# Hybrid S5/MoBA decoder trunk on one core: the 12 table loads of the front in another order and at other steps

## The chip, the core and the metric

One core of a Trainium2 chip runs the whole trunk in one launch. The metric is the device time of the launch in microseconds; lower is better. The engines are named as in the profile: PE is TensorE (PEld its weight loads), DVE is VectorE, ACT is ScalarE, POOL is GpSimd, SP is SyncE, which issues most of the DMAs.

## The reference

Two layers work on x of 256 tokens by 1024 channels in float32. Each layer adds half a SwiGLU feed-forward, then a token mixer, then half a second feed-forward. Layer 0 mixes with a diagonal state-space layer (S5), layer 1 with block-sparse attention.

```python
def swiglu(h, w_gate, w_up, w_down):
    return (jax.nn.silu(h @ w_gate) * (h @ w_up)) @ w_down

for layer in range(DEPTH):
    h = h + 0.5 * swiglu(rms_norm(h, ffn_norm[layer, 0]), ...)
    h = h + mixer(rms_norm(h, mix_norm[layer]))
    h = h + 0.5 * swiglu(rms_norm(h, ffn_norm[layer, 1]), ...)
```

The part of the S5 mixer that matters here doesn't depend on x. Its state matrix, its B (64 groups x 64 states x 16 inputs, real and imaginary) and its C (64 x 16 x 64, real and imaginary) are turned into tables:

```python
    lam_re = mag * jnp.cos(a_im * dt)
    lam_im = mag * jnp.sin(a_im * dt)
    ...
    bb_re, bb_im = cmul(coef_re[..., None], coef_im[..., None], b_re.astype(f32), b_im.astype(f32))
```

## The kernel before

Every product is made of three fp32r matmuls: the activations and the weights are each split into a high part and the remainder, and high x high, high x low and low x high are added up (`mm3`). So each weight is read from DRAM once, as a "raw" tile of 128 x 2048 floats (1 MB), and split by two instructions for each half of it: ACT writes the high part (`whi`, L86) and DVE the rest (`wlo`, L87).

**The stream of weights.** `Stream` holds three raw buffers. The load of a raw is issued on SP's queue as soon as, in program order, the second half of the raw three places before it has been split (`free_raw`, called at the end of `split`); on the chip SP waits there for DVE's `wlo` of that half. Eight, later nine, pairs of split halves may be waiting for TensorE. `pump` splits the next half if a pair of buffers is free and if the raw was issued at least 8 steps ago.

**The first feed-forward.** `ffn` walks over 11 groups of 256 hidden columns. For group j the raws are (j,0) and (j,1), with the gate columns and the up columns of the upper and lower 512 input rows (two DMAs each, L176), and dj, the 256 rows of the down weights (one DMA, L182). For each group there are two products `gu(j, t)` for the two halves t of the tokens, eight steps of three matmuls (L399 to L401) each; behind each of them come ACT's `sg` (L480) and DVE's `act` (L484); `tr(j, t)` transposes the activations on TensorE (L497) in the middle of the next product, and ACT and DVE split them (L499, L500). `dn(j, f)` multiplies by half f of dj's rows into four banks. The order on TensorE is gu(1,0), gu(1,1), dn(0,0), gu(2,0), dn(0,1), gu(2,1), dn(1,0), gu(3,0), dn(1,1), gu(3,1), dn(2,0), and so on.

**The tables, woven in.** `tables` is a generator that builds the S5 tables during the first feed-forward. A clock counts steps: `fill(0.7)` is called before each of the eight steps of a `gu` and after each of the four banks of a `dn`, so a `gu` is 5.6 steps of the clock, a `dn` 2.8 and a whole group 16.8. Each call runs one turn of the loop at the end of `tables`. In a turn, all loads whose entry in `LOADS` is due are issued on SP; one transpose on TensorE is emitted if due (list `later`, from step 44); and the vector work in `work` is emitted if it is due and if the credit of DVE time allows it. All engines run their instructions in program order, so a load is issued behind every load that stands before it in the program.

The 12 loads are: `ld_b4(i, c)`, a quarter c of B, real (i = 0) or imaginary (i = 1), 64 KB in runs of 16 floats, into `bn` (L649); `ld_c2(i, a)`, half of C, 128 KB in runs of 64 floats, into `cn` (L654). Who reads them: `c_tr` transposes C on TensorE (L826), four times, at steps 44.1 to 48.3, and ACT copies the result (`cb`, L829). `b_all` multiplies `bn` by the coefficients on DVE (L628, z<-bn), first at step 49.0 in dn(1,1): one product that reads the real half and one that reads the imaginary half.

Counted out by the clock, the loads stand here before the change (B0r is the first quarter of B, real; C0r the first half of C, real):

| step | place on TensorE | loads |
|---|---|---|
| 16.1, 16.8 | end of gu(1,0) | B0r, B0i; raw d1 is issued after these |
| 17.5 to 19.6 | first four steps of gu(1,1) | B1r, B1i, B2r, B2i, B3r, B3i; raw (3,0) after these |
| 22.4 | end of gu(1,1) | C0r; raw (3,1) after it |
| 24.5, 26.6 | dn(0,0), gu(2,0) | C0i, C1r; raw d2 after them |
| 28.7 | gu(2,0) | C1i; raw (4,0) after it |

After raw (4,0) the kernel issues the second layer norm's gains and the rest of the constants (L290, L291), at step 30.1; then follow raws (4,1), d3, (5,0) at steps 36.4, 39.2 and 42.0.

Of the kernel before, what the change touches and what calls it, by code (L numbers as in the profile page):

```python
# [29 lines left out]
AO = (68, 68, 68, 68)  # L30
OO = 68

LOADS = (16, 16.5, 17, 17.5, 18, 18.5, 19, 19.5, 22, 24, 26, 28)
C_AT, E_AT, B_AT, DENSE, LAG, PACE, AGE = 44, 26, 36, 0.46, 12, 4.0, 8.0


# [84 lines left out]
def trunk_kernel(ctx: ExitStack, tc, x, ffn_norm, ffn_w_gate, ffn_w_up, ffn_w_down, mix_norm,  # L121
# [498 lines left out]
    def tables(tp):  # L620
# [26 lines left out]
        def ld_b4(i, c):  # L647
            b = (s5_b_re, s5_b_im)[i]
            nc.sync.dma_start(bn[i][:, 8 * c:8 * c + 8], bass.AP(tensor=b.tensor, offset=b.offset + 16384 * c,  # L649
                                                                 ap=[[16, 128], [2048, 8], [1, 16]]))  # L650

        def ld_c2(i, a):
            c = (s5_c_re, s5_c_im)[i]
            nc.sync.dma_start(cn[:, i, 4 * a:4 * a + 4], bass.AP(tensor=c.tensor, offset=c.offset + 32768 * a,  # L654
                                                                 ap=[[64, 128], [8192, 4], [1, 64]]))

        loads = [lambda i=i, c=c: ld_b4(i, c) for c in range(4) for i in range(2)]
        loads += [lambda i=i, a=a: ld_c2(i, a) for a in range(2) for i in range(2)]
        yield
        dtb = tp.tile([32, 2, 64], F32, name="dtb")  # L660
        nc.scalar.activation(dtb, ldt[:, :, None].to_broadcast([32, 2, 64]), AF.Exp)
# [258 lines left out]
        done = [-4]  # L920
        dma = list(zip(LOADS, loads))
        credit, then = 0.0, slot[0]
# [404 lines left out]


    tab = tables(tabp) if "s5" in phases else iter(())
    next(tab, None)  # L1330
    slot = [0]
# [145 lines left out]
```

## Time and profile before

| | |
|---|---|
| three runs | 984.52, 984.66, 984.74 us; median 984.66 |
| profiled execution, its own time | 984.45 us |
| its span | 982.5 us |
| granted TensorE clock | 0.999 |
| loads of B on SP | 8, issued from 26.66 to 37.97 us |
| loads of C on SP | 4, issued from 39.82 to 46.26 us |
| the first product with B on DVE | 66.12 us |
| the first transpose of C on TensorE | 56.02 us |

Times of instructions count from the start of the span. The span is what the profile covers; the time of the run has some 2 us around it. A row of a timeline gives start and duration in us, the engine (SPq is SP's queue: the row is the issue of a DMA, not its transfer), the line, the operation, what is written from what, and in brackets how long the engine had been idle and what ended that. Matmuls are pipelined: the rows overlap, and the distance between their starts is what they cost. A row of a DMA list ends with the time from the issue to the landing.

### The profile page before, as it was taken

Reading aid. Unit: us, or ns where it says so; the run is one execution under the profiler, and the core shown is the slowest. Engines: PE = TensorE matmul, PEld = TensorE weight load, DVE = VectorE, ACT = ScalarE, POOL = GpSimd, SP = SyncE. Lnnn points to the kernel's source line nnn. Section 1 sums busy time; section 2 is a strip of 40 time slices with the busy share of each in tenths; the row PEclk is TensorE's granted clock in tenths of the full one; section 3 lists DMA queues with packets and bytes.
Section 4 is the critical chain, followed back from the end, with each engine's and each line's share of the span. In section 5 each row is a group of like instructions: output and inputs, shape, how many; then the busy total and the mean of one; then the engine's idle time right before and its main releaser. Section 6 shows DMA issues by size and latency. Waiting matters only on the chain.

```text
span 982.5 us, 17221 instructions
## 1 busy us (share of the span) xinstructions
PE 972.4 (99%) x6727; PEld 867.2 (88%) x6727; DVE 698.3 (71%) x1118; ACT 559.4 (57%) x1000; POOL 191.6 (19%) x364
## 2 busy tenths in 40 slices
PE   9999999999999999999999999999999999999998
PEld 7878888888888999999999999998788899999997
DVE  5799767769968776666667766665789667766662
ACT  6566766553267555555456655544897656655540
POOL 6963544415711000000010000000441010000000
PEclk9999999999999999999999999999999999999999
DMA  8988877887655666565536756562544546656531
GB/s 282 244 270 274 285 258 239 297 329 242 254 173 173 200 229 208 178 194 192 171 109 216 234 172 214 172 213 92 169 139 164 180 143 215 235 173 213 172 130 43
DMA packets 140001, 198.73 MB, mean 202 GB/s; under 512 B 18232, under 2 KB 111504, under 8 KB 139664
## 3 DMA queue, kind: packets, MB, share of 16 engines
q1 hardware_dynamic: 133808, 184.32, 57.9%
q0 software_dynamic: 5536, 12.71, 3.7%
q8 instruction: 53, 0.87, 0.4%
q10 hardware_dynamic: 576, 0.61, 0.3%
q14 instruction: 28, 0.23, 0.1%
HBM read 183.89 MB, written 13.66 MB: 201 GB/s over the span
## 4 chain that ended last, share of the span: by engine, by line
PE 86%; DVE 5%; issue 2%; POOL 2%; ACT 2%; DMA 2%; SPq 0%; ACTq 0%; DVEq 0%; POOLq 0%
PE pM L554 13%; PE pM L553 13%; PE pM L555 13%; PE pA L399 9%; PE pA L401 9%; PE pA L400 9%; PE pM L399 5%; PE pM L400 5%; PE pM L401 5%; DMA raw<-in_ffn_w_up_dram 2%; PE pA L473 1%; DVE wlo L87 1%; PE pR L333 1%; POOL qrs L306 1%; ACT whi L86 1%
## 5 line engine op out<-in xcount | busy, mean ns | idle before, releaser
L553 PE MATMUL pM<-xa,whi 128*128 128x256 f32 x1056 | 295.7, 280 | 0.0
L554 PE MATMUL pM<-xa,whi 128*128 128x256 f32 x1056 | 294.9, 279 | 0.0
L555 PE MATMUL pM<-xa,wlo 128*128 128x256 f32 x1056 | 294.6, 279 | 0.0
L93 DVE SCALAR_TENSOR_TENSOR wlo<-raw,gT,whi 128x512 fp32r<-128x512 f32 x328 | 228.1, 748 | 70.1 <-ACT whi L92 70.0
L87 DVE TENSOR_TENSOR wlo<-raw,whi 128x1024 fp32r<-128x1024 f32 (+1 forms) x155 | 188.3, 1230 | 56.8 <-ACT whi L86 55.8
L92 ACT ACTIVATE whi<-raw,gT 128x512 fp32r<-128x512 f32 x328 | 213.8, 711 | 15.5 <-PE pA L401 14.4
L554 PEld LDWEIGHTS pM<-xa,whi 128*128 128x128 f32 x1056 | 198.5, 188 | 2.6
L553 PEld LDWEIGHTS pM<-xa,whi 128*128 128x128 f32 x1056 | 198.5, 188 | 2.3
L555 PEld LDWEIGHTS pM<-xa,wlo 128*128 128x128 f32 x1056 | 198.5, 188 | 0.0
L86 ACT ACTIVATE whi<-raw 128x1024 fp32r<-128x1024 f32 (+1 forms) x155 | 158.8, 1049 | 27.0 <-DMA raw<-in_ffn_w_up_dram 10.7
L399 PE MATMUL pA<-whi,ah 128*128 128x512 f32 x352 | 138.8, 394 | 0.0
L400 PE MATMUL pA<-wlo,ah 128*128 128x512 f32 x352 | 137.6, 391 | 0.0
L401 PE MATMUL pA<-whi,al 128*128 128x512 f32 x352 | 137.6, 391 | 0.0
L399 PE MATMUL pM<-whi,xa 128*128 128x512 f32 (+1 forms) x304 | 122.1, 402 | 0.0
L568 ACT ACTIVATE sg<-gr 128x256 f32<-128x256 f32 x66 | 27.6, 418 | 166.1 <-DVE gr L565 166.1
L400 PE MATMUL pM<-wlo,xa 128*128 128x512 f32 (+1 forms) x304 | 115.8, 381 | 0.2
L401 PE MATMUL pM<-whi,xa 128*128 128x512 f32 (+1 forms) x304 | 115.4, 380 | 0.0
L348 POOL TENSOR_TENSOR ms<-ss 128x1 f32<-128x1 f32 x10 | 1.9, 194 | 469.3 <-ACT sq L345 469.3
L401 PEld LDWEIGHTS pA<-whi,al 128*128 128x128 f32 x352 | 66.1, 188 | 14.4
L399 PEld LDWEIGHTS pA<-whi,ah 128*128 128x128 f32 x352 | 66.1, 188 | 11.6
L400 PEld LDWEIGHTS pA<-wlo,ah 128*128 128x128 f32 x352 | 66.2, 188 | 11.3
L565 DVE TENSOR_TENSOR gr<-pM,rrow 128x512 f32<-128x512 f32 x66 | 45.5, 689 | 40.9 <-PE pM L555 40.8
(264 smaller groups left out, 1227.1 us busy)
## 6 DMA issues: line engine op xcount, KB each, us to landing
raw<-in_ffn_w_down_dram SPq DMA_DIRECT2D x44, 1024.0 KB, 5.4
raw<-in_ffn_w_gate_dram SPq DMA_DIRECT2D x80, 512.0 KB, 4.0
raw<-in_ffn_w_up_dram SPq DMA_DIRECT2D x80, 512.0 KB, 5.1
raw<-in_moba_w_qkv_dram SPq DMA_DIRECT2D x12, 1024.0 KB, 5.1
TB<-dB SPq DMA_DIRECT2D x8, 768.0 KB, 7.2
raw<-in_ffn_w_gate_dram SPq DMA_DIRECT2D x16, 256.0 KB, 4.4
raw<-in_ffn_w_up_dram SPq DMA_DIRECT2D x16, 256.0 KB, 4.7
dB<-tt POOLq DMA_DIRECT2D x16, 256.0 KB, 5.0
```

The lines of the kernel that those rows point to most:

```text
L86: nc.scalar.activation(hi[:, c], r[:, c], AF.Copy)
L87: nc.vector.tensor_tensor(lo[:, c], r[:, c], hi[:, c].bitcast(F32), op=OP.subtract)
L92: nc.scalar.activation(hi[:, c], r[:, c], AF.Identity, scale=g)
L93: nc.vector.scalar_tensor_tensor(lo[:, c], r[:, c], g, hi[:, c].bitcast(F32), op0=OP.mult, op1=OP.subtract)
L399: mm(o, xh, wh, start=start, stop=False)
L400: mm(o, xh, wl, start=False, stop=False)
L401: mm(o, xl, wh, start=False, stop=stop)
L553: mm(o, a, xh, start=k == 0 and i == 0, stop=False, skip_group_check=True)
L554: mm(o, a, xl, start=False, stop=False, skip_group_check=True)
L555: mm(o, b, xh, start=False, stop=k == 7, skip_group_check=True)
L565: V.tensor_tensor(gr, ps.rearrange("p (i c) -> p i c", i=2), Rr["row"][:, None, :].to_broadcast([128, 2, 256]), op=OP.mult)
L568: nc.scalar.activation(sg, gr[:, 0, :], AF.Silu)
```

## The change

Two lines: the list of due steps, and the order of the list of loads.

```diff
-LOADS = (16, 16.5, 17, 17.5, 18, 18.5, 19, 19.5, 22, 24, 26, 28)
+LOADS = (22, 24, 26, 28, 30, 32, 34, 36, 38, 40, 42, 44)
 C_AT, E_AT, B_AT, DENSE, LAG, PACE, AGE = 44, 26, 36, 0.46, 12, 4.0, 8.0
...
-        loads = [lambda i=i, c=c: ld_b4(i, c) for c in range(4) for i in range(2)]
-        loads += [lambda i=i, a=a: ld_c2(i, a) for a in range(2) for i in range(2)]
+        loads = [lambda i=i, a=a: ld_c2(i, a) for a in range(2) for i in range(2)]
+        loads += [lambda i=i, c=c: ld_b4(i, c) for c in range(4) for i in range(2)]
```

The steps at which vector work and transposes are emitted don't depend on the loads. Counted out, the four loads of C keep their places (22, 24, 26 and 28 were their entries before), and the eight of B stand here:

| step | place on TensorE | load | its neighbours on SP |
|---|---|---|---|
| 30.1 | gu(2,0) | B0r | after raw (4,0), before the gains and constants |
| 32.2 | dn(0,1) | B0i | |
| 34.3 | gu(2,1) | B1r | |
| 36.4 | gu(2,1) | B1i | before raw (4,1) |
| 38.5 | gu(2,1) | B2r | after raw (4,1), before raw d3 |
| 40.6 | dn(1,0) | B2i | after raw d3 |
| 42.0 | dn(1,0) | B3r | before raw (5,0) |
| 44.1 | gu(3,0) | B3i | after raw (5,0) |

## The prediction

> **What bounds the kernel now.** I read the page's busy shares first, then the stretch tables, then what TensorE waits for, the chain of waits around 38 us, and last single instructions.
>
> ```profile
> PE 972.4 (99%) x6727; PEld 867.2 (88%) x6727; DVE 698.3 (71%) x1118; ACT 559.4 (57%) x1000; POOL 191.6 (19%) x364
> 50.00:75.00 25.00, 24.48 (x117) 19.77 (x118) 24.96 (x40) 16.54 (x26) 15.88 (x27) 1.00 0.82 271
> PE pR L497 <- DVE act L484: 1.0, 1, 1.0
> PE pR L826 <- ACT cb L829: 0.3, 1, 0.3
> ```
>
> TensorE is the bound: 972.4 of 982.5 us. In 50 to 75 us (columns: the stretch, then PE, PEld, DVE, ACT, POOL busy, granted clock, DMA share, GB/s) it is busy for 24.48 of 25.00 at a clock of 1.00, and DVE for 24.96. The change moves only loads, so it can give back no more than TensorE's waits near those loads. There are two:
>
> ```profile
> 48.85 0.39 PE L401 MATMUL pM<-whi,xa 128*128 128x512 f32 x1
> 50.25 0.44 PE L497 MATMUL pR<-cst,act 128*128 128x128 f32 x2 [1.02 <-DVE act L484]
> ...
> 59.40 0.39 PE L401 MATMUL pM<-whi,xa 128*128 128x512 f32 x1
> 59.63 0.38 PE L497 MATMUL pR<-cst,act 128*128 128x128 f32 x2
> 60.28 0.63 PE L826 MATMUL pR<-cst,cn 128*64 128x128 f32 x4 [0.27 <-ACT cb L829]
> ...
> 78.28 0.38 PE L497 MATMUL pR<-cst,act 128*128 128x128 f32 x2
> 78.41 0.48 PE L399 MATMUL pM<-whi,xa 128*128 128x512 f32 x1
> ```
>
> Matmuls start every 0.23 us and overlap, so I count from start to start. The transposes of group 2's activations should start 0.23 us after 48.85 (as 59.63 does after 59.40), at 49.08; they start at 50.25. Lost: 1.17 us. After a transpose pair the next work starts 0.13 us later (78.28 to 78.41); at 60.28 it starts 0.65 us later. Lost: 0.5 us. Together 1.7 us is the most that this stage holds.
>
> What makes the first wait is in the chain of waits:
>
> ```profile
> 38.19 1.03 SPq L176
> 39.27 5.44 DMA raw<-in_ffn_w_up_dram
> 44.79 1.07 ACT whi L86
> 45.88 1.23 DVE wlo L87
> 48.33 1.13 DVE wlo L87
> 49.91 6.76 DMA raw<-in_ffn_w_up_dram
> ```
>
> The raw of group 3, half 0 lands at 44.7. ACT and DVE then work back to back until DVE, in its order, reaches the activation that TensorE wants. A raw that lands x us earlier moves this by x.
>
> **The change part by part.** *B out of 26 to 38 us.*
>
> ```profile
> 26.11 0.51 SPq L176 DMA_DIRECT2D raw<-in_ffn_w_up_dram  x1
> 26.66 0.51 SPq L649 DMA_DIRECT2D bn<-in_s_b_re_dram  x1
> 37.36 0.61 SPq L649 DMA_DIRECT2D bn<-in_s_b_im_dram  x1
> 38.06 1.16 SPq L176 DMA_DIRECT2D raw<-in_ffn_w_gate_dram  x1
> 39.27 0.51 SPq L176 DMA_DIRECT2D raw<-in_ffn_w_up_dram  x1
> ...
> 55.35 0.37 SPq L176 DMA_DIRECT2D raw<-in_ffn_w_gate_dram  x1
> 55.77 0.51 SPq L176 DMA_DIRECT2D raw<-in_ffn_w_up_dram  x1
> ```
> ```profile
> 35.25:39.75 4.50, 4.50 (x22) 3.69 (x21) 4.02 (x6) 3.08 (x4) 4.42 (x8) 1.00 1.03 103
> 41.50:43.25 1.75, 1.75 (x9) 1.42 (x9) 1.72 (x6) 0.00 (x0) 1.59 (x4) 1.00 1.10 380
> 55.00:57.00 2.00, 2.00 (x13) 1.63 (x12) 2.00 (x4) 1.18 (x3) 2.00 (x4) 1.00 0.33 57
> 63.00:65.00 2.00, 2.00 (x12) 1.71 (x11) 2.00 (x4) 0.75 (x2) 0.00 (x0) 1.00 0.14 27
> ```
>
> In 35.25 to 39.75 the DMA engines are full (1.03) and move 103 GB/s: the B loads, in pieces of 64 bytes. With raws alone they move 380. A 64 KB load at 103 GB/s is 0.64 us of all engines, eight are 5.1 us. The raw of (3,0) is asked for at 38.06 into the end of this backlog: its gate issue takes 1.16 us where the one at 55.35 takes 0.37, so its up half is issued at 39.27 and not 0.42 us after the gate, at 38.48. These are landings of one load each, us in the last column: up issued at 39.27; up issued at 55.77, when the DMA engines were nearly idle (0.33); the last B, at 37.36, with only B loads ahead of it; the last C, at 45.70; and the pair at 26.11 and 26.66, a raw's up half and the first B.
>
> ```profile
> raw<-in_ffn_w_up_dram SPq DMA_DIRECT2D x1, 512.0 KB, 5.4
> raw<-in_ffn_w_up_dram SPq DMA_DIRECT2D x1, 512.0 KB, 4.9
> bn<-in_s_b_im_dram SPq DMA_DIRECT2D x1, 64.0 KB, 3.3
> cn<-in_s_c_im_dram SPq DMA_DIRECT2D x1, 128.0 KB, 8.0
> raw<-in_ffn_w_up_dram SPq DMA_DIRECT2D x1, 512.0 KB, 5.5
> bn<-in_s_b_re_dram SPq DMA_DIRECT2D x1, 64.0 KB, 5.5
> ```
>
> Without the backlog: 38.48 + 4.9 = 43.4 instead of 39.27 + 5.4 = 44.7, 1.3 us earlier. The request itself doesn't move: it waits for a split that hangs on TensorE. Lower bound: only the issue is repaired (0.8 us, landing still 5.4; the second rival goes below it); upper bound 1.3. C now comes first but at the places it had, so it is still interleaved with raw (3,1). I take 1.2 us, from which the wait of 1.17 gives **1.1** back (0.8 to 1.17).
>
> [...]
>
> *The second wait.* ACT is held there by raw (4,0), 6.76 us in the chain above, in a DMA stretch that is full until 55. All of it moves up by the same 1.2 us: the split that frees its buffer is DVE's at 48.33, and no B lies ahead of it. But TensorE moves up by 1.1 too. I take **0**; bounds -0.5 (ACT gains more than TensorE) and +0.1.
>
> *B into 50 to 64 us.* By the clock's steps SP's order becomes raw (4,0), B, mix norm and constants, three B, raw (4,1), B, raw d3, two B, raw (5,0), last B.
>
> ```profile
> 51.00 0.42 SPq L291 DMA_DIRECT2D cst<-in_consts_dram  x1
> 63.62 0.37 SPq L176 DMA_DIRECT2D raw<-in_ffn_w_gate_dram  x1
> 65.52 1.06 ACT L86 ACTIVATE whi<-raw 128x1024 fp32r<-128x1024 f32 x1 [1.31 <-PE pA L401]
> ```
>
> SP has nothing to do from 51.42 to 55.35; four issues of 0.6 us fit. Behind them in SP's queue wait raws (4,1), d3 and (5,0). (4,1) lands at 60.7 now and ACT takes it at 65.52, held by TensorE: nearly 5 us of cover, against 2.6 us of B data ahead of it. So these cost **0**; with the cover gone each B would cost its 0.64 us. The DMA engines have room: shares of 0.33 in 55 to 57, 0.14 in 63 to 65.
>
> *The last B is the danger.* It stands behind raw (5,0), which waits for a split on DVE, and the product that reads B (L628, z<-bn) follows that split on the same DVE:
>
> ```profile
> 62.34 1.25 DVE L87 TENSOR_TENSOR wlo<-raw,whi 128x1024 fp32r<-128x1024 f32 x1
> 66.72 0.68 DVE L628 TENSOR_TENSOR z<-bn,ncf 128x512 f32<-128x512 f32 x1
> 74.70 0.47 DVE L484 SCALAR_TENSOR_TENSOR act<-pM,rr,sg 128x256 f32<-128x256 f32 x1
> ```
>
> The split ends at 63.6 and raw (5,0) goes out at 63.62. DVE has hardly a pause from 45.88 to there, so both come 1.2 us earlier, at 62.4. Its up half goes out at 62.8 and lands 4.9 later, at 67.7. A B right behind a raw landed 0.6 us after it: 26.66 + 5.5 = 32.2 against 26.11 + 5.5 = 31.6. So the last B lands at about 68.3, and with the B loads still moving ahead of raw (5,0) I take 68.6. DVE comes to the second product (z<-bn,ncf) at 66.72 - 1.2 = 65.5 and stands for **3.1 us**, a new wait. Queued behind it on DVE are the splits of (4,1) and d3, the other products of B, and at 74.70 group 3's second activation, which TensorE transposes at 78.28. From the second product to that activation's end are 75.17 - 66.72 = 8.45 us of work without a pause: 68.6 + 8.45 = 77.05. TensorE, 1.1 us earlier, wants it at 77.2. The stall just fits. I put **+0.1** on it; lower bound 0 (with 3.3 us, as the last B had, the load lands at 66.6). Upper bound by the last C's 8.0 us: issued at 63.3, landing at 71.3, activation at 79.75, TensorE waits 2.55 us.
>
> C's four loads keep their places, so the transposes that read C (56 us) lose nothing.
>
> **Sum:** -1.1 + 0 + 0 + 0.1 = -1.0 us. The profiled execution took 984.45 (span 982.5, 2.0 around it), so 983.45; the median of the runs is 984.66, 0.2 above, and the forecast is **983.7**.
>
> **The rivals.** *Both waits go.* ACT gets ahead of TensorE, and the last B is early enough: -1.7, 983.0. For it: every load of the stage has less ahead of it. Against: raw (4,0) is held by other raws and C, not by B.
>
> *Nothing was owed to B.* The backlog ended at about 39.75, and a raw asked for at 38.06 moves little before 40 anyway; only the issue is repaired and the interleaved C eats the rest. Gain 0.3: 984.4. Against: the gate issue of 1.16 us.
>
> *The last B is late.* Place: DVE at the second product of B. Price: each us by which it lands after 68.75 is a us for TensorE, and from 69.85 on that outweighs the 1.1 gained. With 8.0 us to land, as the last C, and one more B's 0.64 us ahead of raw (5,0), it lands at 71.95; the sum is -1.1 + 3.2 = +2.1: 986.8. For it: two B and d3 are still to move when raw (5,0) is asked for. Against: the DMA share of 0.14 in 63 to 65, which they have to fill first.
>
> That the loads don't go where the change says is no rival: nothing but the clock's steps places them.
>
> **How the numbers follow.** Forecast 0.48 (own range 983.2 to 984.3), both waits gone 0.10, nothing owed to B 0.10, last B late 0.32. The range takes in the first rival's 983.0 less 0.2, which is the spread of the runs, and the third up to 987.0: **982.8 to 987.0**. A measurement tells about 0.2% (2.0 us) from no change. Faster by that would need more than the 1.7 us that are lost here: 0.05. Slower by that needs the last B after 71.85, a little over half of the third rival: 0.18. Within: 0.77.
>
> **What would show it.** The gate issue of raw (3,0) back at about 0.4 us and its landing near 43.4; TensorE's wait near 50 us gone or under 0.3; the wait at 60 us still there; B issued between 49 and 64 us, its last load behind raw (5,0); a pause of DVE of some 3 us before z<-bn, and TensorE's pair near 77 us with a wait under 0.3. Wrong if that pair waits over a microsecond, or if TensorE still waits at 50 us with raw (3,0) on time.

## Result and profile after

The changed kernel takes **986.51 us** (median of 22 runs, 984.80 to 988.43) beside 984.50 us of the kernel before on the same chip (median of 22, 983.67 to 986.80): a ratio of 1.0018, 95% interval 1.0012 to 1.0024. The forecast was 983.7. The time lies in the range given, on the slower side of no change where the forecast lay on the faster. The profiled execution took 985.17 us with a span of 983.0 and a granted clock of 1.000.

First the page's busy line of the changed kernel, then TensorE's stretches (columns: the stretch, PE, PEld, DVE, ACT, POOL busy, granted clock, DMA share, GB/s) and its list of waits from 25 to 100 us.

```profile
PE 972.6 (99%) x6727; PEld 867.9 (88%) x6727; DVE 698.6 (71%) x1118; ACT 559.6 (57%) x1000; POOL 191.4 (19%) x364
```
```profile
25.00:50.00 25.00, 25.00 (x116) 20.46 (x116) 20.85 (x41) 15.72 (x22) 22.93 (x46) 1.00 0.87 262
50.00:75.00 25.00, 22.80 (x110) 18.33 (x109) 21.36 (x32) 13.51 (x23) 15.54 (x29) 1.00 0.89 227
```
```profile
PE pR L826 <- DVE al L500: 2.2, 1, 2.2
```

The same work is done, and TensorE stays the bound. The two waits of before are gone, the first stretch is full, and there is one new wait of 2.2 us in the second: the transposes of C (L826) wait for DVE's `al` (L500). The timeline shows all three places, and behind them the last B.

```profile
39.86 1.06 ACT L86 ACTIVATE whi<-raw 128x1024 fp32r<-128x1024 f32 x1 [1.67 <-DMA raw<-in_ffn_w_up_dram]
...
49.02 0.38 PE L497 MATMUL pR<-cst,act 128*128 128x128 f32 x2
...
58.35 0.38 PE L497 MATMUL pR<-cst,act 128*128 128x128 f32 x2
58.57 0.60 PE L826 MATMUL pR<-cst,cn 128*64 128x128 f32 x4
...
62.97 0.41 DVE L500 TENSOR_TENSOR al<-pR,ah 128x256 fp32r<-128x256 f32 x1
63.44 0.63 PE L826 MATMUL pR<-cst,cn 128*64 128x128 f32 x4 [2.20 <-DVE al L500]
...
68.72 0.69 DVE L628 TENSOR_TENSOR z<-bn,ncf 128x512 f32<-128x512 f32 x1 [3.63 <-DMA bn<-in_s_b_im_dram]
70.46 0.38 PE L497 MATMUL pR<-cst,act 128*128 128x128 f32 x2
76.69 0.47 DVE L484 SCALAR_TENSOR_TENSOR act<-pM,rr,sg 128x256 f32<-128x256 f32 x1
78.90 0.38 PE L497 MATMUL pR<-cst,act 128*128 128x128 f32 x2
```

Raw (3,0) is split from 39.86 instead of 44.79. Group 2's transposes start at 49.02 instead of 50.25, and the third transpose of C at 58.57 instead of 60.28: up to here TensorE has gained **1.71 us**, all that the stage held. The fourth transpose of C followed the third 2.53 us later before:

```profile
62.81 0.60 PE L826 MATMUL pR<-cst,cn 128*64 128x128 f32 x4
```

By that it would start at 61.1 now. It starts at 63.44 and loses **2.35 us**. What is left is 0.64 us later, and so it stays: group 3's second pair of transposes is at 78.90 instead of 78.28, the span 0.5 us longer, the execution's time 0.72.

The rest of the 2.0 us between the medians isn't in this execution. Of the 22 runs, nine have a granted clock of 0.999 or 1.000 and a median of 985.28; thirteen have 0.997 or 0.998 and a median of 986.80. The experiments come to that below.

### Why the fourth transpose waits

On TensorE, DVE and ACT the two built programs have the same instructions in the same order. What differs beside SP's queue is the place of eight of the 122 small PSUM tiles that `psR()` hands out. There are two buffers for them (`tag="R", bufs=2`), and the framework decides in its own plan of the program which tile gets which. In order of the program, tiles 17 to 24 (counted from 0) have swapped: the fourth transpose of C, the gains' transpose (L295), four transposes of the activations of groups 3 and 4, and two table tiles. These are the buffers, called 0 and 1, of tiles 13 to 19:

| tile | before | after |
|---|---|---|
| 13, C transpose 1 | 1 | 1 |
| 14, C transpose 2 | 0 | 0 |
| 15, tr(2,1) | 1 | 1 |
| 16, C transpose 3 | 0 | 0 |
| 17, C transpose 4 | 0 | 1 |
| 18, gains | 1 | 0 |
| 19, tr(3,0) | 0 | 1 |

Before, the fourth transpose follows the third in one buffer and needs only that ACT has copied that one out (`cb`, which ends at 59.97 in the changed kernel). After, it follows tr(2,1), whose buffer DVE reads in `al` (L500, the remainder of the activations behind ACT's high part); and DVE, in the middle of table work, comes to `al` at 62.97. TensorE is there at 61.1.

### The profile page after: what moved, and what is told of

Read it like the earlier page. It is cut to its first block, busy times and chain, and to the rows that moved or that the text cites. A ratio compares the mean times of both kernels' runs of the same rounds, so it can differ in the third digit from the quotient of the medians.

```text
span 983.0 us, 17225 instructions
## 1 busy us (share of the span) xinstructions
PE 972.6 (99%) x6727; PEld 867.9 (88%) x6727; DVE 698.6 (71%) x1118; ACT 559.6 (57%) x1000; POOL 191.4 (19%) x364
## 4 chain that ended last, share of the span: by engine, by line
PE 86%; DVE 6%; POOL 4%; issue 3%; ACT 2%; POOLq 0%; ACTq 0%; DVEq 0%
PE pM L553 13%; PE pM L554 13%; PE pM L555 13%; PE pA L399 9%; PE pA L401 9%; PE pA L400 9%; PE pM L399 5%; PE pM L400 4%; PE pM L401 4%; DVE wlo L87 1%; PE pR L333 1%; POOL qrs L306 1%; POOL sc L682 1%; PE pR L866 1%; DVE z L628 1%
```

## Experiments

The runs come in three groups, each on a chip of its own with runs of the kernel before in between: first the buffers, then the last B, the first filled wait and the order alone, then the rest. Medians are compared within a group. The starts of the profiled executions lie up to 0.7 us apart (the same issue of a raw stands between 25.01 and 25.70 us in them), so times of two executions are compared as distances where tenths count.

### The PSUM buffers by themselves

Theory: the swapped buffer costs 2.3 us and the loads alone bring 1.0 to 1.7. Rival: the loads themselves (DMA or SP) delay DVE, and the buffer is only where it shows. The buffers are set by hand, with a string that gives each tile its buffer; here that of the kernel before.

```diff
-    def psR():
-        return pp.tile([128, 512], F32, name="pR", tag="R", bufs=2)
+    BANKS = iter("01010101010101010010101010100101011011010101010101010101010101010101010101010101010101010101010101010101010101010101010101")
+    psR = lambda: pp.tile([128, 512], F32, name="pR", tag="R" + next(BANKS), bufs=1)
```

The changed kernel again, unedited:

> The changed kernel once more, to see how its runs spread. Theory PSUM buffer: the loads gave TensorE 1.7 us, and a wait of 2.35 us before the fourth transpose of C (63.44 us) took it back; it comes from which of the two PSUM buffers of tag R that transpose was given. Theory clock: this wait lets the granted clock fall in some executions; those show 0.997 instead of 1.000 and are some 1.4 us longer. Both: median 986 to 987, in two groups near 985.1 and 986.6 that go with the clock. Rival, late B: DVE's pause of 3.6 us before z<-bn costs the time; then the spread has no tie to the clock.

Measured: 985.59 us beside 983.92, ratio 1.0020 (1.0011 to 1.0030). The median is below the 986 to 987 expected, but the two groups are there and go with the clock: five runs at 0.999 or 1.000 with a median of 985.20, four at 0.997 or 0.998 from 986.52 to 986.86.

The kernel before again, unedited:

> The kernel before once more, for the clocks of its runs. Theory clock: its longest wait is 1.17 us, so its runs stay at 0.999 to 1.000 and between 984 and 985; a run above 985.3 would show a lower clock. Rival, spread of another kind: the same share of runs at 0.997 as the changed kernel has.

Measured: 984.18, ratio 1.0001 (0.9992 to 1.0010), every run at 0.999 or 1.000. In this profiled execution the wait for `act` near 50 us is 0.25 us and not 1.02, and two waits for ACT's `cb`, of 0.36 and 0.35 us, follow up to the third transpose. So one profiled execution doesn't say how the loss of this stage is shared out.

The changed kernel with the buffers of before:

> The changed kernel, with the PSUM buffer of every tile of tag R (121 transposes and small products) set by hand to the one it had in the kernel before; eight of them differ, from the fourth transpose of C on. Nothing else differs. PSUM buffer: the wait of 2.35 us at the fourth transpose of C is gone; TensorE then comes 1.7 us earlier than before and may wait 0.6 us for group 3's second activation, which ends at 77.2; span 981.2 to 981.6, runs near 983.4, the clock at 1.000. Late B: span and runs stay at 983.0 and 986.5.

Measured: **982.96**, ratio 0.9994 (0.9985 to 1.0003), which takes in no change. Ten runs lie between 982.59 and 984.16; one took 986.95 at a clock of 0.999, and what held it is not known. The timeline:

```profile
58.49 0.60 PE L826 MATMUL pR<-cst,cn 128*64 128x128 f32 x4
61.00 0.60 PE L826 MATMUL pR<-cst,cn 128*64 128x128 f32 x4
...
67.86 0.69 DVE L628 TENSOR_TENSOR z<-bn,ncf 128x512 f32<-128x512 f32 x1 [2.84 <-DMA bn<-in_s_b_im_dram]
67.98 0.38 PE L497 MATMUL pR<-cst,act 128*128 128x128 f32 x2
75.82 0.48 DVE L484 SCALAR_TENSOR_TENSOR act<-pM,rr,sg 128x256 f32<-128x256 f32 x1
76.43 0.38 PE L497 MATMUL pR<-cst,act 128*128 128x128 f32 x2
```

The kernel before with the buffers of the changed one:

> The kernel before, with the PSUM buffers of tag R set by hand to those of the changed kernel. Loads as before. PSUM buffer: the fourth transpose of C waits from 62.8 for DVE's split (L500) at 64.72 to 65.13, 2.3 us; span 984.8; with the clock falling in some runs 986.6 to 988.2. Late B: span 982.5, runs 984.5.

Measured: **986.96**, ratio 1.0032 (1.0021 to 1.0044). Its timeline:

```profile
59.84 0.63 PE L826 MATMUL pR<-cst,cn 128*64 128x128 f32 x4 [0.35 <-ACT cb L829]
...
63.99 0.41 DVE L500 TENSOR_TENSOR al<-pR,ah 128x256 fp32r<-128x256 f32 x1
64.46 0.63 PE L826 MATMUL pR<-cst,cn 128*64 128x128 f32 x4 [1.94 <-DVE al L500]
```

The wait goes with the buffers and not with the loads. With the buffers of before, the fourth transpose follows the third after 2.51 us without a wait; with those of the changed kernel the old loads show the same wait on `al`. The four medians: old loads 983.92 and 986.96, new loads 982.96 and 985.59. Loads alone: -0.96 (by the interval anything from -1.5 to +0.3) or -1.37. Buffers alone: +3.04 or +2.63. In the traces, up to the fourth transpose and counted from the same raw's issue, the loads alone bring 1.6 us (62.54 - 25.50 in the kernel before of this group, 61.00 - 25.59 here). That is what the theory says for the buffers, and the rival falls; the gain of the loads is clear in the traces and not in this median. Only the +2.6 to +3.0 is more than the 2.35 us of the wait.

### The clock after the wait

The profiled execution of the changed kernel in that group had a granted clock of 0.998. Its stretches, beside two of the first profiled execution of the same kernel:

```profile
62.00:63.00 1.00, 0.23 (x2) 0.23 (x3) 1.00 (x4) 0.00 (x0) 1.00 (x4) 1.00 1.34 186
63.00:64.00 1.00, 1.00 (x7) 0.85 (x6) 0.82 (x3) 0.55 (x2) 0.96 (x4) 0.80 0.51 52
64.00:65.00 1.00, 1.00 (x3) 0.78 (x3) 0.46 (x1) 0.20 (x1) 0.99 (x3) 0.50 0.90 280
65.00:66.00 1.00, 1.00 (x4) 0.76 (x3) 0.29 (x1) 0.00 (x0) 0.53 (x1) 0.50 1.08 375
66.00:67.00 1.00, 1.00 (x4) 0.35 (x2) 0.00 (x0) 0.00 (x0) 0.00 (x0) 0.50 0.97 251
67.00:68.00 1.00, 1.00 (x5) 0.84 (x6) 0.00 (x0) 1.00 (x1) 0.00 (x0) 0.99 0.93 244
```
```profile
64.00:65.00 1.00, 1.00 (x6) 0.84 (x5) 1.00 (x3) 0.76 (x2) 0.97 (x3) 1.00 0.66 182
65.00:66.00 1.00, 1.00 (x5) 0.57 (x4) 0.08 (x1) 0.00 (x0) 0.73 (x3) 1.00 1.08 382
```

After a wait of 1.98 us the clock (the third column from the end) is 0.80, then 0.50 for three microseconds: 0.20 + 3 x 0.50 = 1.7 us of TensorE's time. From 67 to 68 us it is back at 0.99. After a wait of 2.20 us in the other execution it stayed at 1.00. Theory: the pause itself brings the clock down in some executions. To test it, TensorE is given something to do while the transpose waits. The first attempt, with the buffers of the changed kernel set by hand and one place more in the string for the added tile:

```diff
         def c_tr(i, a):
+            if (i, a) == (1, 1):
+                ps = psR()
+                for b in range(9):
+                    mm(ps[:, 0:128], ident, ident, start=True, stop=True)
             ps = psR()
```

> The changed kernel with its own PSUM buffers, and nine matmuls of the constants with themselves, read by nobody, on TensorE ahead of the fourth transpose of C, in the other PSUM buffer: they add work. TensorE then has something to do in most of the 2.2 us in which it waits for DVE's al. Theory, the wait itself lowers the granted clock afterwards in some executions (0.50 for 3 us in one of them): all runs are near 985.1 with a clock of 0.999 or 1.000, and none of 984.9 to 985.4 becomes 986.4 to 988. Rival, the lower clock has another cause than the pause: half of the runs or more are still at 986.4 and above with a clock of 0.997 or 0.998.

Measured: 988.62 us (987.21 to 989.29, five runs) beside 984.28, a miss of the experiment and not of the theory: the string of buffers had given the added tile the buffer that `al` still reads, not the other one, so the nine matmuls waited as well and came on top:

```profile
63.06 2.27 PE L827 MATMUL pR<-cst 128*128 128x128 f32 x18 [2.08 <-DVE al L500]
```

The pause was kept, and so were the two kinds of runs: three of five at a clock of 0.997 or 0.998 (988.62 to 989.29), two at 0.999 (987.21 and 987.29). The second attempt has the added tile in the other buffer, and eight matmuls.

> The changed kernel with its own PSUM buffers, and eight matmuls of the constants with themselves, read by nobody, on TensorE ahead of the fourth transpose of C. This time they go into the other PSUM buffer, the one that ACT has read out by then, so they run while the transpose waits. Nine of them took 2.27 us, eight take some 2.0 us, about the 2.1 us of the wait. Theory, the pause lowers the granted clock afterwards: all runs between 984.8 and 986.0 with a clock of 0.999 or 1.000. Rival, the lower clock has another cause: about half of the runs at 986.3 and above with 0.997 or 0.998.

Measured: 985.25 us (984.96 to 985.78, 11 runs) beside 983.91, ratio 1.0013 (1.0005 to 1.0022). In the timeline the matmuls fill the wait and leave 0.60 us of it:

```profile
60.77 1.95 PE L827 MATMUL pR<-cst 128*128 128x128 f32 x16
63.32 0.63 PE L830 MATMUL pR<-cst,cn 128*64 128x128 f32 x4 [0.60 <-DVE al L500]
```

All 11 runs have a clock of 0.999 or 1.000, and none reaches 986. Of the runs in which the wait stands open, 13 of 22, 4 of 9, 3 of 6 and 3 of 5 had 0.997 or 0.998. The other kernels fit in. The kernel before, whose longest wait in this stretch is 1.02 us, has 0.999 or 1.000 in all 85 runs of the three groups. Below, one run of 11 is under 0.999 with a wait of 1.46 us in the profiled execution, three of 11 with 1.75, four of five with 3.77 and five of five with 5.83; and the profiled execution with the wait of 3.77 us shows 0.65 from 80 to 82 us and 0.50 from 82 to 84 behind it, 2 x 0.35 + 2 x 0.50 = 1.7 us again.

So the pause brings the lower clock, in 23 of the 42 runs in which it stands open, and that costs about 1.5 us (medians of 986.80 and 985.28 in the 22 runs of the result). Why it comes in some executions and not in others isn't shown. With it the buffers' price is whole: 2.35 us of wait, and 1.5 us in about half of the runs. Counted over the runs at 0.999 or 1.000 alone, the buffers cost 2.30 us with the old loads (986.22 beside 983.92) and 2.24 with the new ones (985.20 beside 982.96), which is the wait.

### The order alone and the steps alone

The order of the list alone, at the old steps; the framework's own buffers are then those of before:

```diff
-        loads = [lambda i=i, c=c: ld_b4(i, c) for c in range(4) for i in range(2)]
-        loads += [lambda i=i, a=a: ld_c2(i, a) for a in range(2) for i in range(2)]
+        loads = [lambda i=i, a=a: ld_c2(i, a) for a in range(2) for i in range(2)]
+        loads += [lambda i=i, c=c: ld_b4(i, c) for c in range(4) for i in range(2)]
```

> The kernel before with the new order of the list alone: C first, then B, at the old steps. The framework gives it the PSUM buffers of before. Ahead of raw (3,0) now stand the four loads of C and four of B instead of eight of B; the other four of B stand where C stood. By the forecast's first term raw (3,0) is held by the 64-byte pieces of B ahead of it: with half of them it goes out between the 38.06 of before and the 33.94 of the changed kernel, about 36, TensorE's first wait near 50 us shrinks from 1.17 us to 0 to 0.4, and the time is 983.0 to 983.6 beside some 983.9 of the kernel before. Rival, C's 512 KB weigh as much as B's 256 KB: raw (3,0) at 38, the same wait, the same time.

Measured: 984.53 beside 984.28, ratio 1.0006 (0.9997 to 1.0014). The rival holds:

```profile
37.22 0.53 SPq L176 DMA_DIRECT2D raw<-in_ffn_w_gate_dram  x1
37.79 1.04 SPq L176 DMA_DIRECT2D raw<-in_ffn_w_up_dram  x1
...
44.71 2.01 ACT L86 ACTIVATE whi<-raw 128x1024 fp32r<-128x1024 f32 x2 [7.09 <-DMA raw<-in_ffn_w_up_dram]
...
50.07 0.44 PE L497 MATMUL pR<-cst,act 128*128 128x128 f32 x2 [1.46 <-DVE act L484]
```

Four loads of C and four of B ahead of raw (3,0) hold it nearly as long as eight of B: counted from the raw's issue near 25 us (25.10 here, 25.70 before), it goes out after 12.12 us instead of 12.36 and is split after 19.61 instead of 19.09. TensorE waits no less than it did.

The steps alone, B still first, with the buffers of before set by hand:

```diff
-LOADS = (16, 16.5, 17, 17.5, 18, 18.5, 19, 19.5, 22, 24, 26, 28)
+LOADS = (22, 24, 26, 28, 30, 32, 34, 36, 38, 40, 42, 44)
```

> The kernel before with the new steps alone, B still ahead of C, and the PSUM buffers of before set by hand (the framework's own would differ). C's four loads now stand at steps 38 to 44, the last behind raw (5,0). TensorE's first wait near 50 us is gone as in the changed kernel (-1.0 us), but the transposes that read C, from 54.7 us, wait for loads issued at 54 to 63 us that take 5 us or more: the fourth some 8 to 12 us. Expected 990 to 998 us. Rival, C is early enough or the waits overlap with work: under 986.

Measured: 990.78 beside 983.91, ratio 1.0066 (1.0052 to 1.0080). As in the changed kernel the wait near 50 us is gone, but C is late:

```profile
60.66 1.06 PE L826 MATMUL pR<-cst,cn 128*64 128x128 f32 x4 [5.83 <-DMA cn<-in_s_c_re_dram]
64.61 0.89 PE L826 MATMUL pR<-cst,cn 128*64 128x128 f32 x4 [0.33 <-DMA cn<-in_s_c_re_dram]
```

The time is in the range expected, but by another wait: the first transpose takes nearly all of it, and the fourth, of which 8 to 12 us were expected, didn't wait at all, since its data had landed by then. So the two lines of the change belong together: the steps free raw (3,0), and the order keeps C in time.

### The last load of B

All with the buffers of before. The last B ahead of raw (5,0):

```diff
-LOADS = (22, 24, 26, 28, 30, 32, 34, 36, 38, 40, 42, 44)
+LOADS = (22, 24, 26, 28, 30, 32, 34, 36, 38, 40, 42, 42)
```

> The changed kernel with the PSUM buffers of before, and the last load of B (B3i) ahead of raw (5,0) instead of behind it. The forecast's third term: behind raw (5,0) the load stops DVE, but the stop just fits. By that DVE's pause ahead of z<-bn,ncf (2.84 us with the load behind) goes under 0.5 us, raw (5,0) goes out 0.5 us later with nothing waiting for it, and the time stays within 0.3 us of the 982.96 of the same kernel with the load behind, about 1.0 us under the kernel before. Rival, the late load costs something that the stage hides (TensorE waited 0.20 us there for DVE's act): the time falls by 0.5 us or more.

Measured: **982.99** beside 984.28, ratio 0.9987 (0.9978 to 0.9996). DVE's pause is gone:

```profile
64.97 0.77 DVE L628 TENSOR_TENSOR z<-bn,ncf 128x512 f32<-128x512 f32 x1
...
67.97 0.38 PE L497 MATMUL pR<-cst,act 128*128 128x128 f32 x2
76.41 0.38 PE L497 MATMUL pR<-cst,act 128*128 128x128 f32 x2
```

Three loads of B behind raw (5,0):

```diff
-LOADS = (22, 24, 26, 28, 30, 32, 34, 36, 38, 40, 42, 44)
+LOADS = (22, 24, 26, 28, 30, 32, 34, 36, 38, 44, 44, 44)
```

> The changed kernel with the PSUM buffers of before, and the last three loads of B (B2i, B3r, B3i) behind raw (5,0). The forecast said that each us by which the last B lands after the point where the stall fits is a us for TensorE. With one load behind, z<-bn,ncf started at 67.86 and TensorE took the activation 0.20 us after it wanted it, so the cover is used up. Two loads more of 0.64 us each land the last one 1.3 us later: z<-bn,ncf near 69.1, TensorE's wait ahead of the transposes of group 3's second half near 1.5 us, the time about 1.3 us over the 982.96 with one load behind, near that of the kernel before. Rival, DVE has other work to do in between or a second cover exists: no wait over 0.4 us there and the same 982.9.

Measured: 987.40, ratio 1.0033 (1.0020 to 1.0045). The place is as expected, the size isn't: SP's issue of the last load was itself held for 2.76 us, and the product starts 3.6 us later than with one load behind, not 1.3.

```profile
67.60 0.38 PE L497 MATMUL pR<-cst,act 128*128 128x128 f32 x2
...
71.46 0.69 DVE L628 TENSOR_TENSOR z<-bn,ncf 128x512 f32<-128x512 f32 x1 [0.98 <-DMA bn<-in_s_b_im_dram]
...
79.96 0.44 PE L497 MATMUL pR<-cst,act 128*128 128x128 f32 x2 [3.77 <-DVE act L484]
```

Then both versions of the last B side by side, on the third chip. Ahead of raw (5,0):

> The changed kernel with the PSUM buffers of before and the last B ahead of raw (5,0), beside the same with the last B behind raw (5,0) on the same chip. DVE's pause of 2.8 us was gone here and TensorE's transposes lay 8.44 us apart in both, so the two are equal within 0.3 us, both 0.8 to 1.4 us under the kernel before. Rival, the late load costs in some executions: this one has the lower median by 0.5 us or more.

Measured: **982.64** (982.24 to 982.85) beside 983.91, ratio 0.9985 (0.9976 to 0.9994). Behind it:

> The changed kernel with the PSUM buffers of before, the last B behind raw (5,0) as in the change: 0.8 to 1.3 us under the kernel before (0.96 under it the first time), no TensorE wait over 0.3 us from 25 to 100 us.

Measured: 984.99 (983.04 to 987.34), ratio 1.0013 (1.0004 to 1.0022), two microseconds more than the same kernel on the first chip, beside equal times of the kernel before. The two versions were expected to be equal and are not; the rival, that the late load costs in some executions, holds. Here the load came later, and DVE's pause no longer fitted:

```profile
67.40 0.38 PE L497 MATMUL pR<-cst,act 128*128 128x128 f32 x2
69.24 0.69 DVE L628 TENSOR_TENSOR z<-bn,ncf 128x512 f32<-128x512 f32 x1 [4.33 <-DMA bn<-in_s_b_im_dram]
77.75 0.44 PE L497 MATMUL pR<-cst,act 128*128 128x128 f32 x2 [1.75 <-DVE act L484]
```

It isn't the chip alone. In the second profiled execution of the unedited changed kernel, on the first chip, the load was later still:

```profile
71.65 0.69 DVE L628 TENSOR_TENSOR z<-bn,ncf 128x512 f32<-128x512 f32 x1 [6.36 <-DMA bn<-in_s_b_im_dram]
80.16 0.44 PE L497 MATMUL pR<-cst,act 128*128 128x128 f32 x2 [0.26 <-DVE act L484]
```

Taken together, with the start of the second product counted from group 3's first pair of transposes, and the distance from that pair to the second:

| profiled execution | product starts | second pair after |
|---|---|---|
| last B ahead (first of the two) | -3.00 | 8.44 |
| the changed kernel | -1.74 | 8.44 |
| last B behind, first chip | -0.12 | 8.45 |
| changed kernel, wait filled | +0.30 | 8.80 |
| the changed kernel again, first chip | +0.36 | 8.87 |
| last B behind, third chip | +1.84 | 10.35 |
| three B behind | +3.86 | 12.36 |

Up to the pair's own start the late load is free; from there each microsecond costs TensorE one. With the buffers of before, the last B's issue began 0.7 us later against the pair on the third chip than on the first, and the product started 6.2 us after it instead of 5.0.

Six profiled executions have this one load behind raw (5,0). In all of them the raw's up half, issued just ahead of it, lands 5.1 to 5.6 us after its issue. The last B lands 4.8 to 7.9 us after its own, so 0.3 to 2.9 us behind that raw. It rises with the time that SP was held at the issue of raw (5,0)'s gate half, from 4.8 us at 0.54 to 7.9 us at 1.84:

| profiled execution | gate issue of raw (5,0) held | last B, issue to landing |
|---|---|---|
| last B behind, first chip | 0.54 | 4.8 |
| changed kernel, first filled wait | 0.66 | 4.8 |
| the changed kernel | 1.05 | 5.1 |
| last B behind, third chip | 1.31 | 6.0 |
| changed kernel, wait filled | 1.35 | 6.8 |
| the changed kernel again, first chip | 1.84 | 7.9 |

What lies behind it, a backlog of loads by the author's estimate, isn't shown, nor why it differs from execution to execution. In the changed kernel the buffer's wait of 2.35 us moves the pair back and is cover for the late load: nothing of it shows in the first execution, and 0.26 us in the second.

## Why the prediction was wrong, point by point

- **"The change moves only loads, so it can give back no more than TensorE's waits near those loads."** This is the step that failed. In the source only loads move; in the program eight PSUM tiles change their buffer. The same holds for "C's four loads keep their places, so the transposes that read C (56 us) lose nothing": C's data are in time, and the fourth transpose loses 2.35 us by its output's buffer. None of the rivals had this. The exchange of buffers in both kernels shows it: +2.6 and +3.0 us.
- **B out of 26 to 38 us, -1.1.** The term came out and the wait is gone (1.23 us by the pair's start), but the way to it was not the one given. "The request itself doesn't move: it waits for a split that hangs on TensorE" was wrong, as SP's queue in the changed kernel shows:

```profile
33.94 0.37 SPq L176 DMA_DIRECT2D raw<-in_ffn_w_gate_dram  x1
34.35 0.50 SPq L176 DMA_DIRECT2D raw<-in_ffn_w_up_dram  x1
34.91 0.50 SPq L654 DMA_DIRECT2D cn<-in_s_c_re_dram  x1
```

In the kernel before, the split that frees its buffer is the second of these two, and SP is in the middle of B's issues when it ends:

```profile
31.51 2.44 DVE L87 TENSOR_TENSOR wlo<-raw,whi 128x1024 fp32r<-128x1024 f32 x2
32.44 3.40 SPq L649 DMA_DIRECT2D bn<-in_s_b_re_dram  x1
```

That split ends at 33.9 in both kernels. The request goes out at 33.94 and not at 38.06: before, it stood on SP behind B's issues, one of which took 3.40 us. With four of B and four of C ahead it still stands there until 37.22 (the order alone). So raw (3,0) is split 4.9 us earlier, where a landing 1.3 us earlier was forecast. That the term is near its size is luck: the wait could give back no more than it held.
- **The second wait, 0 taken, bounds -0.5 and +0.1.** It went too, near its lower bound: from 58.35 to 58.57 there are 0.22 us where 0.65 stood. The forecast moved raw (4,0) up by 1.2 us; its gate half goes out at 47.17 instead of 49.50, 2.3 us earlier. Both waits gone is the first rival's -1.7, and 1.71 was measured up to there.
- **B into 50 to 64 us, 0.** Right. With the buffers of before no wait of TensorE is listed from 25 to 100 us on the first chip, though B's issues took up to 1.8 us each in the changed kernel and not 0.6.
- **The last B.** In the first profiled execution nearly to the digit: the last issue at 63.43 (63.3 forecast), the second product at 68.72 (68.6), DVE's pause 3.63 us (3.1), group 3's second activation done at 77.16 (77.05). That closeness is luck. In the second execution of the same kernel the last issue is at 63.56 and the product at 71.65; the forecast had the load land 0.6 us behind the raw, and the runs show 0.3 to 2.9. Its threshold is right: 68.75 is 8.45 us ahead of the 77.2 us at which TensorE wants the second pair, and the first pair starts 8.44 us ahead of the second. So the threshold is the first pair's own start, and the table of starts shows both that point and the price of one microsecond each. Without the swapped buffers the rival "last B late" comes true in part, +1.9 us in one of the two profiled executions with the last B behind; its ground, loads still moving when raw (5,0) is asked for, shows there in the DMA share of 1.03 in 60 to 62 us, with the request at 61.11.
- **The sum.** Against the kernel before on the same chip the loads alone measure -0.96 and +1.08 us, where the forecast had -1.0. The first agrees in the number only: both waits go, not one. The forecast left out +2.35 us for the buffer, and the clock behind it.

The version that beats both kernels is the change with the buffers of before and the last B ahead of raw (5,0): 982.99 and 982.64 us, 0.13 and 0.15% under the kernel before on the same chips.

Left open: by what rule the framework's plan gives the fourth transpose another buffer. The order alone leaves the buffers as they were, and the new steps change them; more wasn't tried.

## What to carry to other kernels

An edit that moves only loads can still move which of two rotating buffers a tile gets. Compare the buffers of two built programs tile by tile, not only the order of their instructions, and where a tile must follow a reader that is early, fix its buffer by name. A load that just fits in one execution can miss by some microseconds in another (the same product started 0.12 us ahead of TensorE's pair on one chip and 1.84 us behind it on another): put the last of a group ahead of the big transfer, not behind it. And a pause of TensorE can cost more than its length: here the clock fell behind a pause of some 2 us in 23 of 42 runs, and these took about 1.5 us more.

## What the runs showed of the hardware

- A pause of TensorE of some 2 us can be followed by a lower granted clock: one trace shows 0.80 and then three times 0.50 in the four stretches of 1 us from 63 to 67 us, behind a pause of 1.98 us that ends at 62.77, and 0.99 in the next; another stays at 1.00 behind 2.20 us. By their mean clock of 0.997 or 0.998 it happened in 23 of 42 runs; with the pause cut to 0.60 us, in none of 11.
- The same load of 64 KB behind the same 1 MB raw landed 4.8 to 7.9 us after its issue in six executions. In two executions of one program, with SP held 1.05 and 1.84 us at the raw's issue just before, it was 5.1 and 7.9 us.
- The issue of one 64 KB load in pieces of 64 bytes held SP's queue for 0.47 to 3.40 us in the kernel before. A 1 MB load that stood behind eight of these in program order went out at 38.06; without them, and ready at the same time, it went out at 33.94.
